# Larger experts in blocks of 1024 columns, gate before up, silu beside the down products

## The chip, the cores and the metric

The program runs on one core of one Trainium2 chip. Its time is the device time of one execution in microseconds (us); three executions of the kernel before gave a median of 1556.11 us (1555.88 to 1558.05). The three lie within 0.14% of each other.

## The reference

A bidirectional encoder of two layers over 256 tokens of width 1024. Each layer mixes the tokens and then applies a channel mixer: dense in layer 0, eight experts with two per token in layer 1. Only the experts matter here:

```python
def swiglu(h, w_gate, w_up, w_down):
    return (jax.nn.silu(h @ w_gate) * (h @ w_up)) @ w_down

def moe_swiglu(h, router, w_gate, w_up, w_down):
    logits = (t @ router); top_val, top_idx = lax.top_k(logits, 2); gates = softmax(top_val)
    combine = sum(one_hot(top_idx, 8) * gates[..., None], axis=1)
    for e in range(8):
        out = out + combine[:, e:e+1] * swiglu(t, w_gate[e], w_up[e], w_down[e])
```

`w_gate` and `w_up` are 1024 x 3584 for each expert, `w_down` is 3584 x 1024, all float32: 44 MB an expert, 352 MB in all, which is four fifths of what the program reads.

## The kernel before, in words

**Order of experts.** The tokens of an expert are gathered by matmuls with one-hot matrices. Experts run in pairs. Slots 0 and 1 are fixed; the other six experts are sorted by size at run time, so that slots 2, 4 and 6 hold at most 64 tokens ("few") and slots 3, 5 and 7 up to 128. Slots 0, 1, 3, 5 and 7 are the "larger" experts of the title. Below, (3, 1) is block 1 of slot 3.

**Loads.** SyncE (SP) issues every weight load, 512 KB each, into a ring of slots of 128 x 1024 floats; a load waits until what the slot held before has been read. A larger expert takes 28 loads of the gate matrix, 28 of up and 28 of down. In `wgu` a load of gate or up is 2 x 128 features by 512 columns, so each row of it in HBM is 2 KB long; a load of down is 128 features by 1024, rows of 4 KB. A few expert already takes 1024 columns at a time.

**Splits.** A larger expert is computed to nearly float32 by three float32r products. `wload` splits each load: ScalarE (ACT) rounds it into `whi` (line 200), VectorE (DVE) subtracts into `wlo` (line 208). There are five buffers of each. `mm3` then issues (x high, w high), (x high, w low), (x low, w high). Each load of a larger expert feeds six matmuls of 512 columns. A few expert uses its loads unsplit (`plain`, line 183) in float32.

**Blocks.** A larger expert goes in seven blocks of 512 columns. `gateup` interleaves gate and up: eight loads, one PSUM bank for each of the two (tag `pg`, four banks). After it come the down products of the block before (`down`, four loads). What lies between is put in by `between(k2)`, called four times in a `gateup`:

- `silu` at step 0: ACT takes silu of the gate bank (line 1650), DVE multiplies by the up bank (line 1651), for the block before
- `turn` at step 2: TensorE (PE) transposes the result in four pieces (line 229)
- `turned` at the first down load: ACT and DVE split the transposed result into `mah` and `mal` (lines 1698, 1699)
- generators in `side`: `combine` adds a finished expert's output to `y` (1742, 1743, 1753; for a few expert 1684, 1693), `gather` collects the tokens of the next pair (1600 to 1603), from block `GC0` = 2 of slots 1, 3 and 5.

PE executes in the order in which the code is written. ACT and DVE are ordered when the program is built: `behind_split` only says that a step may not stand ahead of the split of the newest load. Every engine then executes its own list in order.

Of the kernel before, what the change touches and what calls it, by code (L numbers as in the profile page):

```python
# [98 lines left out]
GC0 = 2  # L99
WARM = (7, 5)  # L100
SILU, TURN, TURNED = 0, 2, 1
ZPOOL = ((0, 0), (0, 1))
LAST = (0, 0, 0)


class K:
# [857 lines left out]
    def outproj(self, l, P, ks, first, last):  # L964
# [23 lines left out]
        if last:  # L988
            self.wn = None
            if l == 0:  # L990
                sq = P.tile([128, D], F32, name="nsq", tag="us")
                fT = self.mc.tile([128, 2, KD, T], F32R, name="fT", tag="G")
                self.norm_start(ROW_FFN + 8 * l, (fT[:, 0], fT[:, 1]))
                half = lambda a: self.norm_part((a,), (("pr", "pr", "pr", "py"), ("pq", "pq", "at", "at"))[a])
                self.ahead.append(self.wload(self.A["ffn_gate"][l // 2].rearrange("(k p) c -> p k c", p=128)[:, 0:2, 0:512], 2, 512))
            else:
                self.norm_start(None, None)
                xT = self.mc.tile([128, KD, T], F32, name="xT", tag="G")
                rt = P.tile([128, 512], F32, name="router", tag="gw")
# [6 lines left out]
                wgu = [self.A[n][l // 2, 0].rearrange("(k p) c -> p k c", p=128) for n in ("exp_gate", "exp_up")]  # L1006
                for n_ in range(NAHEAD):
                    self.early = [nc.gpsimd]
                    self.ahead.append(self.wload(wgu[n_ % 2][:, n_ // 2 * 2:n_ // 2 * 2 + 2, 0:512], 2, 512))
# [337 lines left out]
    def moe(self, l, P):  # L1347
# [47 lines left out]
        NB = DFF // 512  # L1395
# [32 lines left out]
        for n_ in range(len(ahead), XSPLIT + 3):  # L1428
            self.early = [nc.gpsimd if n_ in EPOOL else nc.vector]
            self.lo_after = self.pow if n_ > 3 else None  # L1430
            ahead.append(wgu(0, 0, n_ // 2, n_ % 2))
# [19 lines left out]
        def keep_clock(n):  # L1451

            for _ in range(n):
                self.mm(idle, w0[:, 0, :128], w0[:, 0], start=True, stop=True)
# [80 lines left out]
        def run(places, first):  # L1535
# [73 lines left out]
            def gateup(e, c0, between):  # L1609
                gh, gl, gs = G[e // 2]  # L1610
                bs = [self.bank("pg") for _ in range(2)]
                s0 = (e % 2) * 128 if gs is None else 0
                for k2 in range(KD // 2):
                    for s in range(2):
                        wh, wl = wgu(e, c0, k2, s)
                        for j in range(2):
                            k = 2 * k2 + j
                            self.mm3(bs[s], gh[:, k, s0:s0 + 128], gl[:, k, s0:s0 + 128], wh[:, j], wl[:, j],
                                     k == 0, k == KD - 1, False)
                    between(k2)  # L1620
                return bs

            def gateup_few(e, c0, between):
# [4 lines left out]
                n = 512 if c0 < DFF // 1024 else 256  # L1628
# [14 lines left out]
                return [b[:, :n] for b in bs]  # L1643

            def silu(e, bs):

                n = bs[0].free_size()
                sl = two("msilu", F32)[:, :n]
                rs = RS[e // 2][:, e % 2:e % 2 + 1]
                nc.scalar.activation(sl, bs[0], AF.Silu, scale=rs)  # L1650
                nc.vector.scalar_tensor_tensor(sl, bs[1], rs, sl, op0=ALU.mult, op1=ALU.mult)
                return sl
# [13 lines left out]
            def down_few(e, c0, operand, acc, beside):  # L1666
                n = 4 if c0 < DFF // 1024 else 2
                at = None
                for f in range(2 * n):
                    w = self.plain(wd[expert(e)][:, c0 * 8 + f:c0 * 8 + f + 1], 1, 1024)  # L1670
                    if not f:
                        with self.behind_split():
                            at = operand()
                    h, f_ = f // n, f % n
                    for hf in range(2):
                        self.mm(acc[64 * hf:64 * hf + 64], at[:, f_ * 128 + h * 64:f_ * 128 + h * 64 + 64], w[:, 0, hf * 512:hf * 512 + 512],
                                start=c0 == 0 and f == 0, stop=c0 == DFF // 1024 and f == 2 * n - 1, skip_group_check=True)
                    if f % 2:
                        beside(f // 2)
# [22 lines left out]
            def down(e, c0, operand, acc, beside):  # L1702
                ws = []
                for f in range(4):
                    ws.append(self.wload(wd[expert(e)][:, c0 * 4 + f:c0 * 4 + f + 1], 1, 1024))
                    if f < TURNED - 1:
                        continue
                    if f == TURNED - 1:
                        with self.behind_split():
                            ah, al = operand()  # L1710
                    for f_ in range(f + 1 if f == TURNED - 1 else 1):
                        one_down(f if f > TURNED - 1 else f_, c0, ah, al, acc, ws)
                    beside(f)

            def one_down(f, c0, ah, al, acc, ws):
                wh, wl = ws[f]
                for hf in range(2):
                    self.mm3(acc[hf], ah[:, f * 128:f * 128 + 128], al[:, f * 128:f * 128 + 128],
                             wh[:, 0, hf * 512:hf * 512 + 512], wl[:, 0, hf * 512:hf * 512 + 512],
                             c0 == 0 and f == 0, c0 == NB - 1 and f == 3, False)  # L1720

            def finish(e, c0, operand, accs, side, beside=lambda f: None):
                if few(e):
                    if c0 == 0:
                        accs[e] = self.bank("py")
                    down_few(e, c0, operand, accs[e], beside)
                    if c0 == DFF // 1024:
                        side.append(combine_few(e, accs[e]))
                    return
                if c0 == 0:  # L1730
                    accs[e] = [self.bank("py") for _ in range(2)]
                down(e, c0, operand, accs[e], beside)
                if c0 == NB - 1:
                    side.append(combine(e, accs[e]))
# [20 lines left out]
            def last(f):  # L1755

                if f == LAST[0]:
                    st["s"] = silu(NE - 1, st["n"])
                if f == LAST[1]:
                    st["t2"] = turn(st["s"])  # L1760
                if f == LAST[2]:
                    st["o"] = turned(st["t2"])

# [9 lines left out]
            seq = [(e, c0) for e in range(NE) for c0 in range(DFF // 1024 + 1 if few(e) else NB)]  # L1773
            if first:
                side.append(turns())
            for n_, (e, c0) in enumerate(seq):
                def between(k2):
                    with self.behind_split():
                        side[:] = [g for g in side if next(g, 0) is None]
                        if not n_:  # L1780
                            if first and k2 == GATES:
                                with self.tc.issue_after(self.gl):
                                    gates()
                            return
# [4 lines left out]
                st["n"] = bs = (gateup_few if few(e) else gateup)(e, c0, between)  # L1789
                if n_:  # L1790
                    finish(*seq[n_ - 1], lambda: (turned_few if few(seq[n_ - 1][0]) else turned)(st["t"]), accs, side, last if n_ == len(seq) - 1 else lambda f: None)
                elif first:
                    self.after = None
                st["b"] = bs
# [5 lines left out]
            finish(*seq[-1], lambda: st["o"], accs, side)  # L1800
# [114 lines left out]
```

## Time and profile before

| | |
|---|---|
| median of three runs | 1556.11 us |
| the profiled execution | 1553.22 us, span 1551.4 us |
| PE / DVE / ACT busy over the span | 94% / 65% / 52% |
| granted TensorE clock, mean | 0.978 of full |
| experts | from about 645 us to 1536 us |

A row of the chain of waits is a start, a length and what ran, followed back from the last instruction. A row of the timeline is a start, the length of one or of several, engine, line, operation, output and inputs, and in square brackets how long the engine had been idle and what it had waited for. Matmul ends are modelled; the distance from one start to the next is the real pace.

### The profile page before, as it was taken

How to read it: one execution, taken by the hardware profiler on the slowest of the kernel's cores; microseconds unless marked ns; L12 is line 12 of the kernel's file. 1: busy time of each engine (PE TensorE's matmuls, PEld its weight loads, DVE VectorE, ACT ScalarE, POOL GpSimd, SP SyncE). 2: the span in 40 equal slices, each digit the busy share in tenths (PEclk: the TensorE clock that was granted, in tenths of full speed). 3: DMA queues.
4: the chain of work that ended last, by engine and by line, in shares of the span. 5: the costliest groups of instructions: out<-in, count | busy, mean ns of one | idle time of the engine just before them, and what ended most of it. 6: DMA issues, size and time to landing. Idle time of an engine off the chain costs nothing.

```text
span 1551.4 us, 27151 instructions
## 1 busy us (share of the span) xinstructions
PE 1463.6 (94%) x10215; PEld 1111.4 (72%) x10215; DVE 1003.6 (65%) x1314; ACT 806.2 (52%) x1142; POOL 178.4 (11%) x161
## 2 busy tenths in 40 slices
PE   7799989999998999799999999999998999998996
PEld 6677889999986778688888743588634687435885
DVE  5865665556659746698899720699512898205896
ACT  4545454444445354587878510687302776205785
POOL 2532100000026423300001000001000010000001
PEclk9899999999998899899999999999999999999998
DMA  7322356666543230899999999999999999999991
GB/s 230 104 70 98 109 166 188 186 182 189 163 120 95 70 125 3 310 412 410 338 332 348 353 407 415 410 411 413 403 419 412 410 411 412 389 416 411 410 413 43
DMA packets 172457, 434.67 MB, mean 280 GB/s; under 512 B 14834, under 2 KB 18013, under 8 KB 172317
## 3 DMA queue, kind: packets, MB, share of 16 engines
q1 hardware_dynamic: 170924, 430.74, 74.4%
q8 instruction: 82, 1.34, 0.3%
q0 software_dynamic: 544, 1.12, 0.3%
q10 hardware_dynamic: 848, 0.99, 0.2%
q14 instruction: 59, 0.48, 0.1%
HBM read 431.75 MB, written 1.05 MB: 279 GB/s over the span
## 4 chain that ended last, share of the span: by engine, by line
PE 75%; DVE 9%; DMA 7%; ACT 3%; issue 3%; POOL 1%; ACTq 0%; SPq 0%; DVEq 0%; POOLq 0%
PE ps L225 72%; PE ps L229 3%; DMA r<-in_exp_up 2%; DMA raw<-in_exp_up 2%; DMA r<-in_exp_gate 2%; DVE wlo L208 2%; DVE wlox L208 1%; DMA posi<-in_positions 1%; ACT whi L200 1%; ACT whix L200 0%; DVE AR L655 0%; DMA x<-in_x 0%; DVE us L550 0%; DVE kd L659 0%; ACT Sf L761 0%
## 5 line engine op out<-in xcount | busy, mean ns | idle before, releaser
L208 DVE TENSOR_TENSOR wlo<-r,whi 128x1024 fp32r<-128x1024 f32 x192 | 234.6, 1248 | 42.3 <-ACT whi L200 41.1
L200 ACT CAST whi<-r 128x1024 fp32r<-128x1024 f32 x195 | 201.0, 1056 | 37.5 <-DMA r<-in_exp_gate 19.3
L208 DVE TENSOR_TENSOR wlox<-r,whix 128x1024 fp32r<-128x1024 f32 x120 | 147.1, 1246 | 65.3 <-ACT whix L200 64.2
L200 ACT CAST whi<-raw 128x1024 fp32r<-128x1024 f32 x119 | 124.7, 1052 | 97.4 <-PE ps L225 82.6
L208 DVE TENSOR_TENSOR wlo<-raw,whi 128x1024 fp32r<-128x1024 f32 x104 | 129.7, 1251 | 59.7 <-ACT whi L200 59.3
L200 ACT CAST whix<-r 128x1024 fp32r<-128x1024 f32 x120 | 124.5, 1056 | 36.9 <-DMA r<-in_exp_gate 25.1
L225 PE MATMUL ps<-whi,gf 128*128 128x512 f32 x400 | 137.2, 401 | 1.3 <-ACT whi L200 1.3
L225 PE MATMUL ps<-r,gs 128*64 128x512 f32 (+1 forms) x636 | 130.6, 541 | 2.6 <-DMA r<-in_exp_up 2.5
L225 PE MATMUL ps<-fT,whi 128*128 128x256 f32 x544 | 100.8, 287 | 4.7 <-DVE gu L1306 3.7
L1417 POOL TENSOR_TENSOR xp<-x,xp 128x512 fp32r<-128x512 f32 x12 | 24.3, 2026 | 631.6 <-ACT xp L1416 631.6
L225 PE MATMUL ps<-whix,gf 128*128 128x512 f32 x272 | 93.9, 400 | 2.5 <-ACT whix L200 2.5
L225 PEld LDWEIGHTS ps<-r,gs 128*64 128x64 f32 x636 | 42.8, 136 | 74.1 <-issue 58.3
L225 PEld LDWEIGHTS ps<-whi,gf 128*128 128x128 f32 x400 | 76.6, 191 | 21.9 <-ACT whi L200 2.9
L225 PEld LDWEIGHTS ps<-fT,whi 128*128 128x128 f32 x544 | 86.2, 194 | 6.0 <-issue 4.3
L1663 ACT COPY mah<-ps 128x512 f32<-128x512 f32 (+1 forms) x12 | 6.4, 532 | 143.9 <-PE ps L229 143.9
L225 PE MATMUL ps<-wlo,gf 128*128 128x512 f32 x200 | 79.6, 398 | 1.2 <-DVE wlo L208 1.1
L225 PE MATMUL ps<-fT,wlo 128*128 128x256 f32 x272 | 77.6, 285 | 0.0
L225 PE MATMUL ps<-whi,hT_h 128*128 128x512 f32 x160 | 69.6, 435 | 5.6 <-DVE up L1073 5.5
L208 DVE TENSOR_TENSOR wlox<-raw,whix 128x1024 fp32r<-128x1024 f32 x51 | 63.1, 1242 | 17.5 <-ACT whix L200 16.6
L225 PE MATMUL ps<-r,mah 128*64 128x512 f32 x276 | 64.8, 599 | 2.4 <-DMA r<-in_exp_down 2.0
L225 PE MATMUL ps<-whi,mah 128*128 128x512 f32 x170 | 66.5, 391 | 0.0
L225 PE MATMUL ps<-wlo,mah 128*128 128x512 f32 x170 | 66.4, 390 | 0.0
(468 smaller groups left out, 3400.3 us busy)
## 6 DMA issues: line engine op xcount, KB each, us to landing
r<-in_exp_down SPq DMA_DIRECT2D x178, 512.0 KB, 10.1
r<-in_exp_up SPq DMA_DIRECT2D x172, 512.0 KB, 10.0
r<-in_exp_gate SPq DMA_DIRECT2D x172, 512.0 KB, 10.0
raw<-in_exp_gate SPq DMA_DIRECT2D x43, 512.0 KB, 10.0
raw<-in_exp_up SPq DMA_DIRECT2D x43, 512.0 KB, 9.9
raw<-in_exp_down SPq DMA_DIRECT2D x37, 512.0 KB, 10.0
raw<-in_w_in_first SPq DMA_DIRECT2D x22, 512.0 KB, 4.3
raw<-in_w_in_rest SPq DMA_DIRECT2D x22, 512.0 KB, 3.6
```

The source lines that it names most:

```text
L200: w1 = nc.scalar.copy(hi[:, :a * b], raw[:, :a * b])
L208: w2 = (early or nc.vector).tensor_sub(lo[:, :a * b], raw[:, :a * b], hi[:, :a * b].bitcast(F32))
L225: self.nc.tensor.matmul(out, lhsT, rhs, start=start, stop=stop, skip_group_check=skip_group_check)
L229: self.nc.tensor.transpose(out, in_, ident)
L1417: nc.gpsimd.tensor_sub(xl, xs, xh.bitcast(F32))
L1663: nc.scalar.copy(at, b)
```

## The change

A larger expert goes in three blocks of 1024 columns and one of 512. A block of 1024 computes all of gate first, into two banks, and then all of up, into two more; its loads are 128 features by 1024 columns. `between` is called once every two loads. `silu` of a block no longer stands in the `gateup` after it but directly behind the first load of the down products that follow its own `gateup` (those of the block before); it is now two steps, silu on ACT and `times` on DVE, one of each per bank. The transposes come at steps 0 and 1 of the next `gateup`, the splits of them at steps 1 and 2. `gather` now starts after block 0. Few experts keep their blocks but follow the same order of steps. Line numbers are lower by 3 up to line 1400 or so, and move by up to 20 behind it.

```diff
-        NB = DFF // 512
+        NB = DFF // 1024 + 1
...
-        def wgu(e, c0, k2, s):
+        def wgu(e, c0, s, k):
             if ahead and first_run[0]:
                 return ahead.pop(0)
-            return self.wload((wg, wu)[s][expert(e)][:, 2 * k2:2 * k2 + 2, c0 * 512:c0 * 512 + 512], 2, 512)
+            w = (wg, wu)[s][expert(e)]
+            if c0 < NB - 1:
+                return self.wload(w[:, k:k + 1, c0 * 1024:c0 * 1024 + 1024], 1, 1024)
+            return self.wload(w[:, 2 * k:2 * k + 2, c0 * 1024:c0 * 1024 + 512], 2, 512)
...
             def gateup(e, c0, between):
...
-                bs = [self.bank("pg") for _ in range(2)]
...
-                for k2 in range(KD // 2):
-                    for s in range(2):
-                        wh, wl = wgu(e, c0, k2, s)
+                n = 2 if c0 < NB - 1 else 1
+                bs = st["n"] = [[], []]
+                for s in range(2):
+                    bs[s].extend(self.bank("pg") for _ in range(n))
+                    for i in range(KD * n // 2):
+                        wh, wl = wgu(e, c0, s, i)
                         for j in range(2):
...
+                            k, h = (i, j) if n == 2 else (2 * i + j, 0)
...
+                        if i % 2:
+                            between(s * (KD * n // 4) + i // 2)
...
             def silu(e, bs):
...
+                sls = []
+                for b in bs:
+                    sls.append(two("msilu", F32)[:, :b.free_size()])
+                    nc.scalar.activation(sls[-1], b, AF.Silu, scale=RS[e // 2][:, e % 2:e % 2 + 1])
+                return sls
+
+            def times(e, sls, bs):
+                for sl, b in zip(sls, bs):
+                    nc.vector.scalar_tensor_tensor(sl, b, RS[e // 2][:, e % 2:e % 2 + 1], sl, op0=ALU.mult, op1=ALU.mult)
...
+            def down(e, c0, ops, acc, beside):
+                n = 4 * len(ops)
+                for f in range(n):
+                    wh, wl = self.wload(wd[expert(e)][:, c0 * 8 + f:c0 * 8 + f + 1], 1, 1024)
+                    ah, al = ops[f // 4]
...
                     beside(f)
...
+            def turn_step(e, i):
+
+                if 0 < i <= len(st["s"]):
+                    st["o"].append((turned_few if few(e) else turned)(st["t"]))
+                if i < len(st["s"]):
+                    st["t"] = turn(st["s"][i])
...
-                        if k2 == SILU:
-                            st["s"] = silu(seq[n_ - 1][0], st["b"])
-                        elif k2 == TURN:
-                            st["t"] = turn(st["s"])
+                        if not step:
+                            st["o"] = []
+                        turn_step(seq[n_ - 1][0], step)
+
+                def beside(f):
+                    with self.behind_split():
+                        if not f:
+                            st["s"] = silu(e, st["n"][0])
+                            times(e, st["s"], st["n"][1])
+                        if end and f > 2:
+                            if f == 3:
+                                st["o"] = []
+                            turn_step(e, f - 3)
...
-                if (e, c0) == (NE - 1, GC0):
+                if (e, c0) == (NE - 1, 0):
...
-                if e % 2 and e < NE - 1 and c0 == GC0:
+                if e % 2 and e < NE - 1 and c0 == 0:
                     side.append(gather(e // 2 + 1))
```

How the steps stand on DVE, in slot 0. In these rows `wlo` with a number is the low half of one load in the order of the program, `msilu` the product of silu and up, `ps` a PSUM bank. Before, at block 4: `ps461` is its up bank, last written from load 470; loads 471 to 474 are down loads, 477 and 478 the first of the next block.

```order
L208 TENSOR_TENSOR wlox470_7936<-raw470_7934,whix470_7935 128x1024
L208 TENSOR_TENSOR wlox471_7948<-myh_7946,whix471_7947 128x1024
L1699 TENSOR_TENSOR mal_7499<-ps468_7918,mah_7498 128x512
L208 TENSOR_TENSOR wlo472_7962<-myl_7960,whi472_7961 128x1024
L208 TENSOR_TENSOR wlo473_7974<-r8_7972,whi473_7973 128x1024
L208 TENSOR_TENSOR wlo474_7986<-y_7984,whi474_7985 128x1024
L208 TENSOR_TENSOR wlox477_7999<-y_7984,whix477_7998 128x1024
L208 TENSOR_TENSOR wlox478_8011<-raw478_8009,whix478_8010 128x1024
L1651 SCALAR_TENSOR_TENSOR msilu_7412<-ps461_7844,rs_7291,msilu_7412 128x512
```

The multiplication stands six splits behind the load that last wrote its up bank.

In the change, the same engine at block 2 of slot 0: `ps467` and `ps468` are its two up banks, last written from load 476; load 477 is the first down load.

```order
L205 TENSOR_TENSOR wlo475_7976<-r8_7974,whi475_7975 128x1024
L205 TENSOR_TENSOR wlo476_7988<-y_7986,whi476_7987 128x1024
L205 TENSOR_TENSOR wlox477_7999<-y_7986,whix477_7998 128x1024
L1660 SCALAR_TENSOR_TENSOR msilu_7461<-ps467_7902,rs_7291,msilu_7461 128x512
L1660 SCALAR_TENSOR_TENSOR msilu_7461<-ps468_7903,rs_7291,msilu_7461 128x512
L205 TENSOR_TENSOR wlox478_8015<-raw478_8013,whix478_8014 128x1024
```

The two multiplications stand one split behind that load, and ahead of the split of load 478.

What PE does there in the change: the last three matmuls of each up bank, then the down products of loads 477 and 478.

```order
L222 MATMUL ps467_7902<-whi476_7987,gl0_7218 128x512
L222 MATMUL ps468_7903<-whi476_7987,gh0_7217 128x512
L222 MATMUL ps468_7903<-wlo476_7988,gh0_7217 128x512
L222 MATMUL ps468_7903<-whi476_7987,gl0_7218 128x512
L222 MATMUL ps445_7688<-whix477_7998,mah_7539 128x512
L222 MATMUL ps445_7688<-wlox477_7999,mah_7539 128x512
L222 MATMUL ps445_7688<-whix477_7998,mal_7540 128x512
L222 MATMUL ps446_7689<-whix477_7998,mah_7539 128x512
L222 MATMUL ps446_7689<-wlox477_7999,mah_7539 128x512
L222 MATMUL ps446_7689<-whix477_7998,mal_7540 128x512
L222 MATMUL ps445_7688<-whix478_8014,mah_7539 128x512
L222 MATMUL ps445_7688<-wlox478_8015,mah_7539 128x512
```

Where `ps461` was followed by four down loads and two of the next block before its multiplication was due, the second matmul of load 478 now needs a split that stands behind the multiplications. In block 1 of slot 0 (and of slots 3, 5 and 7) three splits stand ahead of them instead of one:

```order
L205 TENSOR_TENSOR wlox444_7678<-r19_7676,whix444_7677 128x1024
L205 TENSOR_TENSOR wlox447_7692<-r18_7690,whix447_7691 128x1024
L205 TENSOR_TENSOR wlo448_7708<-r1_7706,whi448_7707 128x1024
L205 TENSOR_TENSOR wlo449_7720<-r2_7718,whi449_7719 128x1024
L1660 SCALAR_TENSOR_TENSOR msilu_7461<-ps435_7595,rs_7291,msilu_7461 128x512
```

Here load 444 was the last of up, and the multiplication moved behind the splits of the down loads 447 to 449.

## Rows read from the trace of the kernel before

**Rows 1.** The page: span, busy times of the engines, GB/s in 40 slices.

```profile
span 1551.4 us, 27151 instructions
PE 1463.6 (94%) x10215; PEld 1111.4 (72%) x10215; DVE 1003.6 (65%) x1314; ACT 806.2 (52%) x1142; POOL 178.4 (11%) x161
GB/s 230 104 70 98 109 166 188 186 182 189 163 120 95 70 125 3 310 412 410 338 332 348 353 407 415 410 411 413 403 419 412 410 411 412 389 416 411 410 413 43
```

**Rows 2.** Windows: length, busy PE, PEld, DVE, ACT, POOL; clock; DMA share; GB/s.

```profile
660.00:760.00 100.00, 100.00 (x454) 82.71 (x453) 91.57 (x92) 80.72 (x86) 0.00 (x0) 1.00 1.04 411
760.00:900.00 140.00, 139.47 (x649) 108.90 (x649) 116.18 (x116) 96.22 (x122) 9.76 (x4) 1.00 0.93 332
900.00:950.00 50.00, 50.00 (x228) 19.24 (x226) 10.63 (x13) 7.24 (x11) 0.00 (x0) 1.00 1.03 419
1100.00:1120.00 20.00, 20.00 (x98) 9.01 (x97) 6.52 (x8) 5.54 (x7) 0.00 (x0) 1.00 1.01 388
```

**Rows 3.** The timeline of PE at the start of slot 3.

```profile
975.54 0.50 PE L225 MATMUL ps<-wlo,gf 128*128 128x512 f32 x1 [0.76 <-DVE wlo L208]
...
1004.14 0.66 PE L229 MATMUL ps<-ident,msilu 128*128 128x128 f32 x4 [0.84 <-DVE y L1693]
```

**Rows 4.** The chain of waits in the experts: start, length, what ran.

```profile
669.62 16.38 PE ps L225 x72
...
719.63 0.44 PE ps L229 x4
...
963.28 9.88 DMA r<-in_exp_gate
...
992.49 0.69 ACT msilu L1650
```

**Rows 5.** The timeline of DVE in slot 0.

```profile
720.72 0.69 DVE L1699 TENSOR_TENSOR mal<-ps,mah 128x512 fp32r<-128x512 f32 x1 [1.47 <-ACT mah L1698]
721.66 1.23 DVE L208 TENSOR_TENSOR wlo<-myl,whi 128x1024 fp32r<-128x1024 f32 x1 [0.25 <-ACT whi L200]
722.81 1.22 DVE L208 TENSOR_TENSOR wlo<-r,whi 128x1024 fp32r<-128x1024 f32 x1
```

**Rows 6.** The timeline of ACT in slot 0.

```profile
728.32 1.06 ACT L200 CAST whi<-r 128x1024 fp32r<-128x1024 f32 x1 [0.30 <-PE ps L225]
```

**Rows 7.** Issues on SP at the end of slot 2; of exp_gate from the page.

```profile
953.00 1.63 SPq L183 DMA_DIRECT2D r<-in_exp_down  x2
...
963.28 0.38 SPq L197 DMA_DIRECT2D r<-in_exp_gate  x1
...
973.28 4.18 SPq L183 DMA_DIRECT2D r<-in_exp_down  x4
...
r<-in_exp_gate SPq DMA_DIRECT2D x172, 512.0 KB, 10.0
```

**Rows 8.** The timeline of PE in the last block of slot 7.

```profile
1524.17 0.39 PE L225 MATMUL ps<-whix,gf 128*128 128x512 f32 x1
...
1525.76 0.60 PE L229 MATMUL ps<-ident,msilu 128*128 128x128 f32 x4
1526.11 0.47 PE L225 MATMUL ps<-whi,mah 128*128 128x512 f32 x1
1526.60 0.50 PE L225 MATMUL ps<-wlo,mah 128*128 128x512 f32 x1
```

**Rows 9.** The timeline of DVE at the same place.

```profile
1524.66 0.75 DVE L1651 SCALAR_TENSOR_TENSOR msilu<-ps,rs,msilu 128x512 f32<-128x512 f32 x1 [1.54 <-PE ps L225]
1525.33 2.35 DVE L208 TENSOR_TENSOR wlo<-r,whi 128x1024 fp32r<-128x1024 f32 x2
```

**Rows 10.** The timeline of PE in the first block of slot 0.

```profile
650.52 0.61 PE L225 MATMUL ps<-sel,one 128*128 128x8 f32 x4 [1.06 <-DVE rs L1571]
```

**Rows 11.** Windows behind that wait and behind the one of rows 3.

```profile
652.00:656.00 4.00, 4.00 (x12) 3.18 (x11) 3.24 (x11) 1.64 (x2) 0.00 (x0) 0.57 1.04 407
1004.00:1008.00 4.00, 3.86 (x19) 3.27 (x20) 4.00 (x6) 2.88 (x4) 0.00 (x0) 1.00 1.06 409
```

More of the change, by code (lines that the diff above doesn't have):

```diff
@@ L98 @@
 GSTEP, GATES = 4, 1
-GC0 = 2
 WARM = (7, 5)
-SILU, TURN, TURNED = 0, 2, 1
 ZPOOL = ((0, 0), (0, 1))
-LAST = (0, 0, 0)
 class K:
@@ L1005, in outproj @@
                 nc.gpsimd.tensor_mul(rt[:, :, :NE], rt[:, :, :NE], gain[:, :, None].to_broadcast([128, KD, NE]))
-                wgu = [self.A[n][l // 2, 0].rearrange("(k p) c -> p k c", p=128) for n in ("exp_gate", "exp_up")]
+                wgu = [self.A["exp_gate"][l // 2, 0].rearrange("(k p) c -> p k c", p=128)]
                 for n_ in range(NAHEAD):
                     self.early = [nc.gpsimd]
-                    self.ahead.append(self.wload(wgu[n_ % 2][:, n_ // 2 * 2:n_ // 2 * 2 + 2, 0:512], 2, 512))
+                    self.ahead.append(self.wload(wgu[0][:, n_:n_ + 1, 0:1024], 1, 1024))
                 lt = self.bank("py")
@@ L1430, in moe @@
             self.lo_after = self.pow if n_ > 3 else None
-            ahead.append(wgu(0, 0, n_ // 2, n_ % 2))
+            ahead.append(wgu(0, 0, 0, n_))
             if n_ == 3:
@@ L1453, in keep_clock @@
             for _ in range(n):
-                self.mm(idle, w0[:, 0, :128], w0[:, 0], start=True, stop=True)
+                self.mm(idle, w0[:, 0, :128], w0[:, 0, :512], start=True, stop=True)
         keep_clock(WARM[0])
@@ L1627, in gateup_few @@
                 bs = [self.bank("pg") for _ in range(2)]
-                n = 512 if c0 < DFF // 1024 else 256
+                n = 512 if c0 < NB - 1 else 256
+                st["n"] = [[b[:, :n]] for b in bs]
                 for k2 in range(KD // 2):
@@ L1664, in turned_few, with down_few @@
                 return at
-            def down_few(e, c0, operand, acc, beside):
-                n = 4 if c0 < DFF // 1024 else 2
-                at = None
+            def down_few(e, c0, ops, acc, beside):
+                n = 4 if c0 < NB - 1 else 2
                 for f in range(2 * n):
                     w = self.plain(wd[expert(e)][:, c0 * 8 + f:c0 * 8 + f + 1], 1, 1024)
-                    if not f:
-                        with self.behind_split():
-                            at = operand()
                     h, f_ = f // n, f % n
                     for hf in range(2):
[L1676 to L1679, printed above, removed]
+                        self.mm(acc[64 * hf:64 * hf + 64], ops[0][:, f_ * 128 + h * 64:f_ * 128 + h * 64 + 64], w[:, 0, hf * 512:hf * 512 + 512],
+                                start=c0 == 0 and f == 0, stop=c0 == NB - 1 and f == 2 * n - 1, skip_group_check=True)
+                    beside(f)
             def combine_few(e, acc):
@@ L1700, in turned @@
                 return ah, al
[L1702 to L1712, printed above, removed]
-                    beside(f)
@@ L1715, in one_down @@
[L1715 to L1729, printed above, removed]
+            def down(e, c0, ops, acc, beside):
[3 more added lines that the diff above has]
+                    ah, al = ops[f // 4]
+                    f_ = slice(f % 4 * 128, f % 4 * 128 + 128)
+                    for hf in range(2):
+                        self.mm3(acc[hf], ah[:, f_], al[:, f_], wh[:, 0, hf * 512:hf * 512 + 512], wl[:, 0, hf * 512:hf * 512 + 512],
+                                 c0 == 0 and f == 0, c0 == NB - 1 and f == n - 1, False)
+                    beside(f)
@@ L1730, in finish @@
+            def finish(e, c0, ops, accs, side, beside=lambda f: None):
                 if c0 == 0:
-                    accs[e] = [self.bank("py") for _ in range(2)]
-                down(e, c0, operand, accs[e], beside)
+                    accs[e] = self.bank("py") if few(e) else [self.bank("py") for _ in range(2)]
+                (down_few if few(e) else down)(e, c0, ops, accs[e], beside)
                 if c0 == NB - 1:
-                    side.append(combine(e, accs[e]))
+                    side.append((combine_few if few(e) else combine)(e, accs[e]))
@@ L1754, in combine @@
                         yield
[L1755 to L1762, printed above, removed]
             G = {}
@@ L1772, in run, with between @@
             accs, st = {}, {}
-            seq = [(e, c0) for e in range(NE) for c0 in range(DFF // 1024 + 1 if few(e) else NB)]
+            seq = [(e, c0) for e in range(NE) for c0 in range(NB)]
             if first:
                 side.append(turns())
+            def turn_step(e, i):
[3 more added lines that the diff above has]
+                    st["t"] = turn(st["s"][i])
             for n_, (e, c0) in enumerate(seq):
-                def between(k2):
+                end = n_ == len(seq) - 1
+                def between(step):
                     with self.behind_split():
@@ L1780, in between @@
                         if not n_:
-                            if first and k2 == GATES:
+                            if first and step == GATES:
                                 with self.tc.issue_after(self.gl):
                                     gates()
+                            if step == KD - 2:
+                                st["s"] = silu(e, st["n"][0])
                             return
-                        if k2 == SILU:
-                            st["s"] = silu(seq[n_ - 1][0], st["b"])
-                        elif k2 == TURN:
-                            st["t"] = turn(st["s"])
@@ L1789, in run @@
-                st["n"] = bs = (gateup_few if few(e) else gateup)(e, c0, between)
-                if n_:
[L1791 to L1794, printed above, removed]
-                if (e, c0) == (NE - 1, GC0):
+                        if not step:
+                            st["o"] = []
+                        turn_step(seq[n_ - 1][0], step)
@@ new lines, in beside @@
+                def beside(f):
+                    with self.behind_split():
+                        if not f:
+                            st["s"] = silu(e, st["n"][0])
+                            times(e, st["s"], st["n"][1])
[3 more added lines that the diff above has]
+                            turn_step(e, f - 3)
+                (gateup_few if few(e) else gateup)(e, c0, between)
+                if n_:
+                    finish(*seq[n_ - 1], st["o"], accs, side, beside)
+                else:
+                    with self.behind_split():
+                        times(e, st["s"], st["n"][1])
+                    if first:
+                        self.after = None
```

17 lines of the change are left out of this document (4 added, 13 removed).

## The prediction, written before the change was run

> **What bounds the kernel now.** I read the page first, then windows along the experts, the chain of waits, and last the timelines of PE, DVE, ACT and SP where the change moves steps. PE is busy 94% of the span and the transfers run at 410 GB/s in most slices of the experts [rows 1], so the share of busy time doesn't say which of the two ends last. The windows do [rows 2]. In 660 to 760 PE has no gap, and the transfers run at 411 GB/s. In 760 to 900 (slots 0 and 1, both larger) PE still has only half a microsecond of gap in 140, and the transfers fall to 332: the ring is full and SP waits for PE. In 900 to 950 (slot 2, few) they are back at 419; PE is shown busy all the time, but it works as loads land: at 975.54, early in slot 3, a split was late for it [rows 3], and the chain goes through a landing of exp_gate that took 9.88 us at 963.28 [rows 4]. In 1100 to 1120 (end of slot 3) the rate dips to 388: the ring is full again, just.
>
> So from the end of a few expert to the moment at which the ring is full the time is PE's, from there to the end of the next few expert it is the transfers'. What PE loses while the larger expert runs is lost for good, as long as the ring is full when that expert ends. A gain of the transfers counts only behind that point, which is in a few expert.
>
> PE's own pace: 72 matmuls in 16.38 us in the chain [rows 4] are 0.2275 us each, so 6 x 0.2275 = 1.365 us a load. DVE makes a split in 722.81 - 721.66 = 1.15 us [rows 5], and ACT stands idle 0.30 us for PE ahead of a split [rows 6]: both run ahead until the five buffers are full. With 1.365 - 1.15 = 0.21 us won a load, it takes DVE five loads or so to win back one lost microsecond.
>
> **What doesn't change.** The number of matmuls, splits, transposes, silus and bytes is the same. 240 of the 280 loads of gate and up have rows of 4 KB where they had 2 KB.
>
> **The rows of the loads.** An issue on SP waits for the load eight before it (10.0 us from issue to landing [rows 7]). The issues at 953.00, 963.28 and 973.28 are eight loads apart: 10.28/8 = 1.285 us for those of 2 KB, 10.00/8 = 1.250 for those of 4 KB. 240 x 0.035 = 8.4 us of transfer go. But the stretches that the transfers limit hold mainly loads of few experts, which keep their form, and the larger expert beside them has PE as its limit. I take 0; the ends are 0 and -8.4.
>
> The Trainium skill (DMA: Bandwidth & Descriptors, Specifications) says that a transfer goes at line rate from 512 bytes on; by that this term is 0 at both ends. The trace shows 0.035 us of difference a load instead, in one pair of issues [rows 7].
>
> **The added wait, the main term.** `times` is now on DVE behind the split of the first down load and ahead of that of the second. It needs the last matmul of up; DVE has run ahead, and stands. Behind it stand the splits, and for the first of them PE comes 7 matmuls after that last matmul of up (six of the first down load, one of the second). Before, six splits stood between, and nothing waited.
>
> The trace has this order once: in the last block, where `last` already put silu behind the first down load. The last matmul of up starts at 1524.17 [rows 8] and so ends at 1524.40; the multiplication starts 0.27 us later at 1524.66, after 1.54 us of idle for PE, and the split stands behind it at 1525.33 [rows 9], 0.67 on. PE goes on with that split at 1526.60 [rows 8]. Wanted it was at 1524.40 + 7 x 0.2275 = 1525.99: 0.61 us late. A block of 1024 has two multiplications, one more by 0.67, but its first bank is done three matmuls (0.68 us) earlier: 0.61 again. If both wait for the end, 0.67 more in the seven wide ones of the places below, +4.7 in all. Lower end: 0, if the transfers set the time there anyway; a gain is excluded, since no work leaves PE.
>
> Where it holds, by the changed order of DVE: in (0,2), (0,3), (1,0), (1,1), (1,2), (1,3), (2,0), and in (3,2), (3,3), (4,0) and the like of slots 5 and 6, and (7,2), (7,3). That is 7 + 3 + 3 + 2 = 15 places. In block 1 of slots 0, 3, 5 and 7 three splits stand ahead of the multiplications, so PE has 19 matmuls (4.3 us) where 2.8 are needed: nothing. In (3,0), (5,0) and (7,0) the down loads are of a few expert and are not split. 15 x 0.61 = +9.2 us.
>
> **Turned.** The split of the transposed result stands two loads ahead of its use. In the trace the transposes end at 719.63 + 0.44 = 720.07 [rows 4], `mal` starts at 720.72 after 1.47 us of idle, and the second split behind it starts at 721.66 + 1.15 = 722.81 [rows 5]. The first split behind `mal` ends at 721.66 + 1.23 = 722.89, so 2.82 us after the transposes. PE now comes for it after two loads and a matmul, 2 x 1.365 + 0.2275 = 2.96. It fits, by 0.14 us. I take 0; if it is missed by as much, 19 blocks x 0.14 = +2.7. A gain isn't there.
>
> **Gather and combine.** `gather` starts in block 1, not 3, and now meets `combine` of the expert before in (1,1), (3,1) and (5,1). The trace shows nothing of the two together. Nearest is a wait of PE for the `y` of combine, 0.84 us at 1004.14 [rows 3]. I take half of it, 3 x 0.4 = +1.2; the ends are 0 and two such waits each, 3 x 2 x 0.84 = +5.0.
>
> **Silu leaves the valley.** At the start of slots 3, 5 and 7, where PE has nothing in hand, the silu of the few expert's last block is in the chain (0.69 us at 992.49 [rows 4]). It now runs earlier, under down loads. I take 3 x -0.7 = -2.1; ends 0 and -3. In the last block the transposes no longer stand between two down loads; the wait behind them, 1526.60 - (1526.11 + 0.23) = 0.26 us [rows 8], goes: -0.3. The four banks of a wide block are all free again one or two loads into the down products, ahead of the next gate: 0.
>
> **Sum.** 9.2 + 0 + 0 + 1.2 - 2.1 - 0.3 = +8.0. The profiled execution took 1553.22 us, so 1561.2; the median of the three runs stands 2.9 above it: 1564.1 us.
>
> **Rivals.** What can be told from no change here is about 0.2%, 3.1 us.
>
> *Faster: the transfers set the time all along.* Then PE's stalls vanish in the ring, and 8.4 us of the loads come back: 1556.1 - 8.4 = 1547.7. For it speaks the rate of 410 or more in nearly every slice of the second half [rows 1]; against it 332 GB/s over 140 us with PE full, and the dip to 388 [rows 2].
>
> *No change: stalls count only in slots 0 and 1.* The dip to 388 is so shallow that in slots 3 to 7 the ring may not be full at the end. Then 7 places stay, 4.3 - 2.1 - 0.3 + 0.4 = +2.3: 1558.4.
>
> *Much slower: the clock.* After the wait of 1.06 us at 650.52 [rows 10] PE had a granted clock of 0.57 on average in 652 to 656 (between the levels of 1.2 and 2.4 GHz): 12 matmuls took 4.00 us [rows 11] where 12 x 0.2275 = 2.73 do, 1.3 us lost. If each of the 15 stalls brought this: 15 x 1.3 = 19 more, 1583. Against it, behind the wait of 0.84 at 1004.14 [rows 3] the granted clock stayed at 1.00 [rows 11], the level of 2.4 GHz. The Trainium skill (TensorE: Matmul & The Clock Gate, "A second HAM failure mode: psum-queue depth-cycling") tells of a kernel whose clock swung because PE idled briefly between groups of matmuls; by it the 1583 would be the forecast, by the second window of rows 11 it is not.
>
> *Slower by more: the stalls are longer.* Both multiplications wait for the end (+4.7) and `turned` is missed (+2.7): 1571.5. The row of the tail has one multiplication, so it can't exclude this.
>
> **How the numbers follow.** Forecast 0.52; faster 0.18; no change 0.18; longer stalls 0.08; clock 0.04. The forecast's own range is 1560 to 1570. It and the two slower rivals make slower, 0.52 + 0.08 + 0.04 = 0.64; faster 0.18, same 0.18. The range from 1549 to 1573 takes in the no-change case and the longer stalls, and all but the end of the faster one; it leaves out the clock.
>
> **What would show it.** *The wait:* rows of the multiplication on DVE with idle time put down to PE, behind them PE idle about 0.6 us for a `wlo` at the 15 places, and PE no longer full in 660 to 760. The chain should then show DVE's msilu and wlo between the matmuls. *The ring:* the time from the start of slot 0 to the end of slot 1 longer by some 4 us, the few experts as long as before. *Turned:* no idle of PE at the first down load of a block. *The loads:* eight issues of gate loads 10.0 us apart also in slot 3. The forecast is wrong if PE shows no idle at those places, if such idle is there but the start of slot 2 stands where it stood, or if the time from slot 3 on shrinks by more than slots 0 and 1 lose.

## The result, and the profile after

The changed kernel took 1568.15 us (median of 6 runs, 1562.98 to 1573.37) beside 1557.07 us for the kernel before: a ratio of 1.0066 (ratios here are those of the means; the medians differ by 11.1 us), 95% interval 1.0046 to 1.0085, or 7 to 13 us more. The forecast was 8.0 us more, 1564, in a range of 1549 to 1573. In a second set of runs the same kernel came out at 1.0055 (1.0042 to 1.0068), 6.5 to 10.6 us.

The page of the kernel after: span, PE, and GB/s in 40 slices.

```profile
span 1561.9 us, 27150 instructions
PE 1466.1 (94%) x10215; PEld 1111.1 (71%) x10215; DVE 1000.7 (64%) x1314; ACT 812.2 (52%) x1142; POOL 177.1 (11%) x161
GB/s 227 106 70 97 108 162 182 185 187 189 162 112 101 69 124 3 321 419 417 287 324 349 342 395 415 419 419 415 355 419 416 420 416 396 393 416 419 419 416 40
```

PE still shows 94% [rows 1], and its 10215 matmuls are the same; from such shares the loss can't be read. The windows answer to [rows 2]. The kernel after reaches the same place in the program 4 to 12.5 us later than the kernel before, so the second and third window end where the few expert's first matmul begins, in slot 2 and in slot 4. The kernel after:

```profile
660.00:760.00 100.00, 99.08 (x446) 81.04 (x445) 88.87 (x93) 80.01 (x85) 0.00 (x0) 1.00 1.03 417
763.85:896.91 133.06, 130.55 (x601) 106.18 (x599) 115.82 (x116) 97.10 (x120) 10.61 (x4) 1.00 0.88 312
1094.10:1114.10 20.00, 19.54 (x87) 15.53 (x87) 15.74 (x16) 12.23 (x14) 0.00 (x0) 1.00 0.94 337
```

The second and third in the kernel before:

```profile
760.00:886.84 126.84, 126.31 (x582) 103.55 (x580) 114.79 (x114) 94.20 (x118) 9.76 (x4) 1.00 0.93 329
1081.60:1101.60 20.00, 20.00 (x95) 16.41 (x93) 16.92 (x18) 12.67 (x18) 3.06 (x1) 1.00 1.03 417
```

PE has gaps where it had none: 0.92 us in the first window (0.00 before), 2.51 in the second (0.53 before), while the transfers, with a full ring, wait more than before (312 GB/s for 329, and at the end of slot 3 337 for 417).

The gap at one of the 15 places, block 2 of slot 0. PE, timeline, columns as in [rows 8]; the `whi,gl` is the last matmul of up:

```profile
731.78 0.39 PE L222 MATMUL ps<-whi,gl 128*128 128x512 f32 x1
...
733.36 0.39 PE L222 MATMUL ps<-whix,mah 128*128 128x512 f32 x1
734.21 0.50 PE L222 MATMUL ps<-wlox,mah 128*128 128x512 f32 x1 [0.46 <-DVE wlox L205]
734.55 0.40 PE L222 MATMUL ps<-whix,mal 128*128 128x512 f32 x1
```

DVE at the same place:

```profile
731.59 1.43 DVE L1660 SCALAR_TENSOR_TENSOR msilu<-ps,rs,msilu 128x512 f32<-128x512 f32 x2 [2.51 <-PE ps L222]
732.94 1.21 DVE L205 TENSOR_TENSOR wlox<-raw,whix 128x1024 fp32r<-128x1024 f32 x1
```

And the chain of waits there:

```profile
731.59 0.64 DVE msilu L1660
...
732.94 1.22 DVE wlox L205
734.16 0.04 issue
734.21 12.35 PE ps L222 x53
```

DVE has run ahead, stands 2.51 us, multiplies twice, and only then makes the split. It begins the split 0.93 us after the last matmul of up (731.78 + 0.23 = 732.01), as in the tail of before: 1525.33 - 1524.40 = 0.93 [rows 8, 9]. From one start to the next PE takes 734.21 - 733.36 = 0.85 us, 0.62 more than its pace of 0.23; the step behind it is 0.34 instead of 0.23, a further 0.11. PE shows such a step of `wlo` in the down products at 15 places: 11 of 0.62, one of 0.72, and three of 0.48 at the first blocks of slots 2, 4 and 6. The sum is 8.98 us, or 10.6 with the 0.11 behind each.

Where the 10.5 us between the two profiled spans stand is read from PE's first matmul of slots 0, 3, 5 and 7 and the first of the last combine. In the kernel before:

```profile
645.17 0.50 PE L225 MATMUL ps<-whi,gh 128*128 128x512 f32 x1 [0.52 <-DVE gl L1603]
974.28 0.50 PE L225 MATMUL ps<-whi,gf 128*128 128x512 f32 x1 [1.29 <-ACT whi L200]
1189.30 0.51 PE L225 MATMUL ps<-whix,gf 128*128 128x512 f32 x1 [1.24 <-ACT whix L200]
1405.47 0.50 PE L225 MATMUL ps<-whix,gf 128*128 128x512 f32 x1 [1.24 <-ACT whix L200]
1536.34 0.50 PE L225 MATMUL ps<-myh,PT 128*128 128x512 f32 x1
```

In the kernel after:

```profile
649.02 0.50 PE L222 MATMUL ps<-whi,gh 128*128 128x512 f32 x1 [0.52 <-DVE gl L1604]
984.56 0.50 PE L222 MATMUL ps<-whi,gf 128*128 128x512 f32 x1 [1.26 <-ACT whi L197]
1202.04 0.50 PE L222 MATMUL ps<-whix,gf 128*128 128x512 f32 x1 [1.24 <-ACT whix L197]
1417.36 0.49 PE L222 MATMUL ps<-whix,gf 128*128 128x512 f32 x1 [1.21 <-ACT whix L197]
1547.69 0.50 PE L222 MATMUL ps<-myh,PT 128*128 128x512 f32 x1
```

The differences are +3.9 ahead of the experts, +6.4 in slots 0 to 2, +2.5 in 3 and 4, -0.9 in 5 and 6, -0.5 in 7, and -0.9 behind. Two of these are not the change's waits. The first lies in the dense stage, where the clock falls at other places from run to run; in the ten traces the experts start between 645.17 and 651.32, at 645.97 to 650.03 with the change's early loads and at 645.17 to 651.32 with those of before. And in slots 5 and 7 the granted clock fell in the kernel before but not after (0.72 against 1.00, the mean of 6 us). The windows of the kernel before there:

```profile
1190.00:1196.00 6.00, 5.44 (x17) 4.32 (x18) 5.85 (x7) 5.01 (x7) 0.00 (x0) 0.72 1.05 411
1406.00:1412.00 6.00, 5.27 (x16) 4.23 (x17) 5.80 (x7) 5.20 (x6) 0.00 (x0) 0.72 1.05 404
```

Those of the kernel after:

```profile
1203.00:1209.00 6.00, 5.70 (x26) 4.60 (x26) 5.17 (x6) 4.92 (x7) 0.00 (x0) 1.00 1.02 418
1418.00:1424.00 6.00, 5.38 (x25) 4.42 (x26) 5.16 (x5) 4.93 (x7) 0.00 (x0) 1.00 1.02 417
```

The matmuls went 0.43 apart in place of 0.23 for 3.4 us there, at a granted clock of 0.50 (1.2 GHz), so such a drop costs about 1.7 us by estimate. Stages are compared below only where both or neither had one.

### The profile page after: what moved, and what is told of

Same layout as the page of the kernel before. It is cut to its first block, busy times and chain, and to the rows that moved or that the text cites. A ratio compares the mean times of both kernels' runs of the same rounds, so it can differ in the third digit from the quotient of the medians.

```text
span 1561.9 us, 27150 instructions
## 1 busy us (share of the span) xinstructions
PE 1466.1 (94%) x10215; PEld 1111.1 (71%) x10215; DVE 1000.7 (64%) x1314; ACT 812.2 (52%) x1142; POOL 177.1 (11%) x161
## 4 chain that ended last, share of the span: by engine, by line
PE 71%; DVE 11%; DMA 9%; ACT 3%; issue 3%; POOL 2%; ACTq 0%; SPq 0%; DVEq 0%; POOLq 0%
PE ps L222 69%; DMA r<-in_exp_up 4%; DVE wlo L205 3%; DMA r<-in_exp_gate 3%; PE ps L226 2%; DVE wlox L205 2%; DMA posi<-in_positions 1%; DMA raw<-in_exp_gate 1%; ACT whi L197 1%; DMA raw<-in_exp_down 1%; ACT whix L197 0%; DVE kd L656 0%; DMA x<-in_x 0%; ACT Sf L758 0%; DVE us L546 0%
## 5 line engine op out<-in xcount | busy, mean ns | idle before, releaser
L197 ACT CAST whi<-r 128x1024 fp32r<-128x1024 f32 x199 | 206.0, 1056 | 47.7 <-DMA r<-in_exp_gate 23.0
L197 ACT CAST whi<-raw 128x1024 fp32r<-128x1024 f32 x115 | 120.8, 1052 | 100.3 <-PE ps L222 88.4
L205 DVE TENSOR_TENSOR wlox<-r,whix 128x1024 fp32r<-128x1024 f32 x119 | 143.8, 1229 | 25.5 <-ACT whix L197 24.8
L222 PE MATMUL ps<-whi,gf 128*128 128x512 f32 x392 | 132.8, 399 | 1.3 <-ACT whi L197 1.3
L1660 DVE SCALAR_TENSOR_TENSOR msilu<-ps,rs,msilu 128x512 f32<-128x512 f32 (+1 forms) x47 | 33.2, 732 | 123.6 <-PE ps L222 74.8
L1655 ACT ACTIVATE msilu<-ps,rs 128x512 f32<-128x512 f32 (+1 forms) x47 | 30.1, 676 | 101.7 <-PE ps L222 101.7
L197 ACT CAST whix<-raw 128x1024 fp32r<-128x1024 f32 x52 | 54.7, 1054 | 23.8 <-PE ps L222 23.4
```

The lines of the kernel that those rows point to most:

```text
L197: w1 = nc.scalar.copy(hi[:, :a * b], raw[:, :a * b])
L205: w2 = (early or nc.vector).tensor_sub(lo[:, :a * b], raw[:, :a * b], hi[:, :a * b].bitcast(F32))
L222: self.nc.tensor.matmul(out, lhsT, rhs, start=start, stop=stop, skip_group_check=skip_group_check)
L1655: nc.scalar.activation(sls[-1], b, AF.Silu, scale=RS[e // 2][:, e % 2:e % 2 + 1])
L1660: nc.vector.scalar_tensor_tensor(sl, b, RS[e // 2][:, e % 2:e % 2 + 1], sl, op0=ALU.mult, op1=ALU.mult)
```

## The experiments

Eight kernels ran, each beside the kernel before: 1, 2, 3 and 7 on one chip, where the kernel before took 1555.98 us, and 4, 5, 6 and 8 on another, where it took 1556.40. The ratios go to the kernel before on the same chip.

**1. The changed kernel again.** No edit.

> The changed kernel once more, unaltered, as the standard of this chip. Theory (waits of DVE): about 10 us above the kernel before (1.0066), with PE standing 0.62 us for a split at 12 places of slots 0, 1, 3, 5 and 7 and 0.48 at the three first blocks of the few experts. The first expert started 3.9 us later than before in the profile of the changed kernel, in code that the change hardly touches. Theory (clock, by chance): that start lies now on this side, now on that of 645 us. Rival (the early loads of the first expert cost time): it lies near 649 again, and near 645 in the kernels that load it as before.

1564.62 us, 1.0055 (1.0042 to 1.0068). The trace has the same 15 places, 8.98 us in sum. Its experts start at 647.61, between the two values, and kernels 3, 7 and 8, with the loads of before, start at 649.60 to 651.32. So the early loads are out as the reason.

**2. Silu behind the third down load.**

```diff
-                        if not f:
+                        if f == 2:
                             st["s"] = silu(e, st["n"][0])
```

> The changed kernel with silu and its multiplication put in behind the third down load in place of the first. Theory (the wait on DVE makes the loss): the places have three splits ahead of the multiplication, PE comes for the fourth 4.3 us after the last product of up, the 15 gaps go and the time falls by 15 x 0.61 = 9.2 us against the changed kernel, to within 2 us of the kernel before. Rival (wide blocks, the two-step turn or the earlier gather make it): it stays some 10 us above the kernel before. Rival (ring): half of it goes, since only the stalls of slots 0 and 1 count.

1555.74 us, 1.0004 (0.9992 to 1.0016): 8.9 us less than the changed kernel beside it (7.9 by the two ratios), and no different from the kernel before. Blocks of 1024, the turn in two steps and the earlier gather are all still there, so together they are not the loss. Groups of PE's instructions in the experts (line, names, count | busy, mean ns | idle before, releaser), in the kernel after:

```profile
L222 PE MATMUL ps<-wlo,mah 128*128 128x512 f32 x161 | 63.8, 397 | 3.7 <-DVE wlo L205 3.7
...
L222 PE MATMUL ps<-wlox,mah 128*128 128x512 f32 x108 | 42.8, 396 | 2.9 <-DVE wlox L205 2.9
```

In this one:

```profile
L222 PE MATMUL ps<-wlo,mah 128*128 128x512 f32 x168 | 65.6, 391 | 0.1
...
L222 PE MATMUL ps<-wlox,mah 128*128 128x512 f32 x112 | 43.6, 389 | 0.0
```

The idle time ahead of `wlo` in the down products, 6.6 us, is gone (0.1; the row's idle is smaller than the step because the ends of matmuls are modelled). One place keeps a step 0.3 us too long, in (1,2) at 860.23. On DVE the multiplications of block 2 no longer wait:

```profile
728.96 1.22 DVE L205 TENSOR_TENSOR wlo<-r,whi 128x1024 fp32r<-128x1024 f32 x1
730.11 1.40 DVE L1660 SCALAR_TENSOR_TENSOR msilu<-ps,rs,msilu 128x512 f32<-128x512 f32 x2
731.43 2.35 DVE L205 TENSOR_TENSOR wlo<-r,whi 128x1024 fp32r<-128x1024 f32 x2
```

**3. The kernel before with silu behind the first down load.**

```diff
+                def early(f):
+                    if f == 0:
+                        with self.behind_split():
+                            st["m"] = silu(e, st["n"])
...
-                            st["s"] = silu(seq[n_ - 1][0], st["b"])
+                            st["s"] = st["m"] if n_ > 1 else silu(seq[n_ - 1][0], st["b"])
...
-    finish(..., last if n_ == len(seq) - 1 else lambda f: None)
+    finish(..., last if n_ == len(seq) - 1 else early)
```

> The kernel before, with blocks of 512 and its own loads, but silu and its multiplication moved behind the first down load for every block. Theory (the place of the multiplication alone makes the loss): by the order on DVE 23 places more have one split ahead of it, 23 x 0.61 = 14 us, less 2 for silu leaving the chain of the valleys: 12 us slower than the kernel before. Rival (the loss comes from the wide blocks or the other loads): within 3 us of the kernel before. Rival (clock): more than 25 us slower.

1570.46 us, 1.0091 (1.0077 to 1.0106), 12 to 16.5 us: the place of the multiplication alone, with neither wide blocks nor new loads. The trace has 23 places more, 14.6 us in sum (21 of them at 0.47 to 0.62, one of 0.75, one of 1.20). One of them on PE:

```profile
745.31 0.39 PE L225 MATMUL ps<-whi,mah 128*128 128x512 f32 x1
746.16 0.50 PE L225 MATMUL ps<-wlo,mah 128*128 128x512 f32 x1 [0.46 <-DVE wlo L208]
```

And on DVE:

```profile
744.22 0.75 DVE L1651 SCALAR_TENSOR_TENSOR msilu<-ps,rs,msilu 128x512 f32<-128x512 f32 x1 [1.53 <-PE ps L225]
744.89 1.21 DVE L208 TENSOR_TENSOR wlo<-r,whi 128x1024 fp32r<-128x1024 f32 x1
```

With one multiplication the step is the same 0.85 us (746.16 - 745.31) as with two in the wide blocks: the first of two does run while the second bank is being finished.

**4. A second DVE instruction in the wait.**

```diff
                     nc.vector.scalar_tensor_tensor(sl, b, ..., sl, op0=ALU.mult, op1=ALU.mult)
+                    nc.vector.tensor_tensor(sl, sl, sl, op=ALU.max)
```

> The changed kernel with one more DVE instruction of 128 x 512 behind each multiplication (a maximum of the product with itself, which leaves the values as they are). Theory (PE waits for what stands on DVE ahead of the split): each stall grows by the instruction, about 0.6 us, in 8 places, and by two of them, 1.2 us, in the 7 places of wide blocks: 13 us slower than the changed kernel, with gaps of 1.2 and 1.8 us on PE. Rival (the gap is the trip from PE to DVE and back, whatever DVE does): the gaps stay at 0.62 and the time within 2 us of the changed kernel.

1569.08 us, 1.0080 (1.0061 to 1.0099); against the changed kernel (1.0055) 4 us more, not 13. In six of the seven wide blocks the step grew as expected (in (1,1) by half of it). Block 2 of slot 0 on PE:

```profile
734.70 0.39 PE L222 MATMUL ps<-whix,mah 128*128 128x512 f32 x1
736.75 0.50 PE L222 MATMUL ps<-wlox,mah 128*128 128x512 f32 x1 [1.67 <-DVE wlox L205]
```

And on DVE:

```profile
732.93 1.43 DVE L1660 SCALAR_TENSOR_TENSOR msilu<-ps,rs,msilu 128x512 f32<-128x512 f32 x2 [2.52 <-PE ps L222]
734.28 1.28 DVE L1661 TENSOR_TENSOR msilu<-msilu 128x512 f32<-128x512 f32 x2
735.48 1.22 DVE L205 TENSOR_TENSOR wlox<-raw,whix 128x1024 fp32r<-128x1024 f32 x1
```

2.05 - 0.23 = 1.82 us late, 1.20 more than 0.62, and the two maxima take 735.48 - 734.28 = 1.20. So PE waits for whatever DVE has ahead of the split, and the trip there and back is not the price. The miss of the time has its reason in the order on DVE: in the narrow blocks the maximum was put behind the next split, and in three of them the multiplication too slipped one split back, where PE waits no more. The steps sum to 16.5 us, 7.5 more, which the interval of the difference of the two ratios (0.3 to 7.5 us) only just holds.

**5 and 6. The wait left in one half.** Silu behind the third down load in slots 0 to 2, and in slots 3 to 7.

```diff
-                        if not f:
+                        if f == (2 if e < 2 or (e, c0) == (2, 0) else 0):    # 5
+                        if f == (0 if e < 2 or (e, c0) == (2, 0) else 2):    # 6
```

> The changed kernel with silu and its multiplication behind the third down load in slots 0, 1 and at the first block of slot 2 only; the 8 places of slots 3 to 7 keep the wait. Theory (every stall counts, as PE fills the ring in each larger expert): those 8 stalls are 6 x 0.62 + 2 x 0.48 = 4.7 us, and with the 0.11 that the matmul behind each adds some 5.5: 5 us slower than the kernel before and 4 faster than the changed kernel. Rival (the ring hides stalls in slots 3 to 7): the same as the kernel before.

> The complement: the wait stays at the 7 places of slots 0 to 2, and goes in slots 3 to 7. Theory: 4.3 us of stalls, with 0.11 each behind them 5: some 5 us slower than the kernel before. Rival (the ring hides stalls in slots 3 to 7): all of the loss stays, 9 us.

Kernel 5 took 1558.41 us, 1.0015 (0.9999 to 1.0032); kernel 6 1559.35, 1.0020 (1.0006 to 1.0034). Both lie below the 5 us expected, which is at the edge of either interval. All nine microseconds in slots 0 to 2 are excluded by kernel 6; that the stalls of 3 to 7 are free is not excluded by the time of kernel 5 alone. The lengths of the stages, from PE's starts as above, are sharper, though each is of one trace (us; * with a drop of the clock):

| | slots 0-2 | 3, 4 | 5, 6 | 7 |
|---|---|---|---|---|
| before | 329.11* | 215.02* | 216.17* | 130.87* |
| after | 335.54* | 217.48* | 215.32 | 130.33 |
| 2, no wait | 329.25 | 215.26* | 215.10* | 130.39* |
| 5, wait in 3 to 7 | 331.68* | 215.50 | 216.69* | 131.74* |
| 6, wait in 0 to 2 | 335.44* | 215.98* | 214.91* | 130.36* |

Like with like: slots 0 to 2, 6 less 5, 3.8 us for steps of 4.0; slots 3 and 4, after less 2, 2.2 for steps of 1.7 and 0.3 behind them; slots 5 and 6, 5 less 2, 1.6 for 1.7; slot 7, 5 less 2, 1.35 for 1.24 and 0.2. Where two traces have the same program and the same clock, a stage differs by up to 0.7 us (slots 3 and 4 of 2 and 6). Within that the steps count in full, in the later slots too; whether the 0.11 behind each counts can't be told.

**7 and 8. The old loads.** Wide blocks with loads of 256 features by 512 columns, first with the wait, then with silu behind the third down load.

```diff
...
-                return self.wload(w[:, k:k + 1, c0 * 1024:c0 * 1024 + 1024], 1, 1024)
+                c = c0 * 1024 + k % 2 * 512
+                return self.wload(w[:, k // 2 * 2:k // 2 * 2 + 2, c:c + 512], 2, 512)
...
```

> The changed kernel, but the wide blocks load 256 features by 512 columns again (rows of 2 KB), the two halves of a block in turn; all else as changed, the waits too. Theory (the row width is worth nothing, since PE sets the time where these loads stand): the same as the changed kernel within 2 us. Rival (4 KB rows gain 0.035 us a load and hide a larger loss): 8.4 us slower than the changed kernel.

> The changed kernel with silu behind the third down load and with loads of 256 features by 512 columns (rows of 2 KB) in the wide blocks: against the same with 4 KB rows it differs in the loads alone, with no wait left in either. Theory (PE sets the time where these loads stand): the same within 1.5 us. Rival (0.035 us a load count): 8.4 us slower than with 4 KB rows.

7 took 1562.70 us, 1.0042 (1.0029 to 1.0055): 1.9 less than the changed kernel, inside the 2 expected, but for a reason that was not foreseen. Only 11 of the 15 places are left, 6.5 us: in (0,2), (1,1), (3,2) and (5,2) the second of the two multiplications came one split later. 8 has no such difference and decides: 1557.15 us, 1.0003 (0.9990 to 1.0015), beside 1.0004 for kernel 2. The 8.4 us of the rival are out: the difference of the two ratios is 0 within 2.7 us. The transfers do go faster with rows of 4 KB; in the first full slice of slot 0 (the 18th) kernel 2 moves 419 GB/s, kernel 8 410. The row of the page, kernel 2:

```profile
GB/s 231 104 71 97 109 169 183 188 183 186 162 117 97 57 138 2 290 419 416 318 347 333 353 403 416 419 420 415 379 419 416 419 415 405 391 416 419 419 413 35
```

Kernel 8:

```profile
GB/s 226 108 69 98 109 163 182 186 188 189 164 106 95 70 138 2 268 410 413 331 341 336 359 391 416 410 410 414 403 418 411 411 410 418 402 416 410 410 415 50
```

The stages show what the times can't. In the order of the table they are 334.75*, 215.48, 215.17 and 131.94* us in kernel 7 and 331.11*, 215.22, 215.20 and 129.44 in kernel 8. In slots 0 to 2 the stalls of 7 count: 3.6 us for steps of 2.8 and 0.5 behind them. In slots 3 to 6 they do not: 0.3 and 0.0 us, for steps of 1.1 and 0.2 behind them in either pair. In kernel 8, with rows of 2 KB, the ring is not full there when the larger expert ends: in the 20 us ahead of slot 4's first matmul the transfers of kernel 2 are held back a little, those of kernel 8 are not (ahead of slot 6 it is 393 and 419 GB/s). So what PE lost could come back in the few expert. With more stalls they count again: in kernel 3, with rows of 2 KB and ten stalls in those slots, 4.7 us of 6.2. A window of kernel 2:

```profile
1086.30:1106.30 20.00, 20.00 (x94) 16.34 (x93) 16.42 (x16) 12.89 (x15) 0.00 (x0) 1.00 1.02 404
```

Of kernel 8:

```profile
1089.80:1109.80 20.00, 20.00 (x92) 16.39 (x92) 16.48 (x16) 12.95 (x15) 0.00 (x0) 1.00 1.03 419
```

And in slots 3 to 6 kernel 8 without a drop of the clock takes as long as kernel 2 with one. So where the clock does not fall, the wider rows may be worth up to the 1.7 us of a drop in either pair of slots; with one trace each this is not shown.

## Why the prediction was right

- **What bounds the kernel.** Right for the changed kernel: stalls of PE in a larger expert are lost in full (5 and 6), and faster loads beside it gain nothing that the times show (8). The stretch from slot 0's first matmul to slot 1's last down product takes 268.49 us, 263.18 before: 5.3 more, where some 4 were expected. But the prediction took loads and stalls as separate terms, and they hang together: its condition, a full ring when the larger expert ends, is met in slots 3 to 6 with the rows of 4 KB, and with those of 2 KB it is not, unless more stalls hold PE up (8 and 7, against 3). The 2% that the loads gain, 419 to 410 GB/s, stand beside the 2.8% that the pair of issues gave, 1.285 to 1.250. The Trainium skill (DMA: Bandwidth & Descriptors, Specifications) has every transfer from 512 bytes on at line rate; in rate the traces differ from that (419 to 410), and in time no run shows a difference.
- **The added wait, +9.2.** Right in place, count and price: 15 places; 0.62 us where 0.61 was expected, though 0.48 at the few experts, where PE's step from the first down product to the second is 0.33 in place of 0.23 (911.54 to 911.87) and PE so comes later for the split; 8.98 in sum. Left out was the slower step behind each (0.11, some 1.7 together). The upper end for wide blocks (+4.7) isn't reached.
- **Turned, 0.** Right: no place of the first down loads shows a gap for it.
- **Silu out of the valley, gather, tail: -1.2 together.** Not tested one by one. Kernel 2 less before, at the same clock, is +0.2, -1.1 and -0.5 in slots 3 to 7, -1.3, where -1.6 was expected of these slots. The meeting of gather and combine shows up as a wait of PE for `rs`, 0.25 us at 876.04 and once more each in slots 3 and 5; the wait of 0.84 us for `y` is in both kernels. What silu in the valley cost PE is a wait of 0.30 us at three places of the kernel before, a step of 0.69 for 0.23, and in the kernel after it is gone: 0.46 each, where 0.7 was taken. The first of them:

```profile
995.43 0.50 PE L225 MATMUL ps<-wlo,gf 128*128 128x512 f32 x1 [0.30 <-DVE wlo L208]
```

- **Not foreseen: some 2 us in slots 0 to 2.** With no wait, these take 331.7 (5) at the clock of before, which took 329.1. About 1.0 of them lies behind the last down product of slot 1 (66.9 us to the first matmul of slot 3 in kernel 2, 65.9 before and 65.8 in kernel 3); between the two one load more lands (47 for 46) in every kernel with blocks of 1024. Why is open. Kernel 2 is still no slower than before as a whole.
- **Rivals.** Faster by the loads: out (8). No change since the ring hides the later stalls: out by the stages for the changed kernel, though so it is in slots 3 to 6 with the old loads (7). Clock: out; in ten traces no stall of 0.6 to 1.8 us in the larger experts is followed by a drop. The swing that the Trainium skill (TensorE: Matmul & The Clock Gate, "A second HAM failure mode: psum-queue depth-cycling") tells of is shown by no run here at such stalls. Longer stalls: out, with 0.62 in the wide blocks and none for `turned`.

The size came out larger in the first runs (10.3 us) than in the second (8.6); the sum of 8.0 stands inside either interval.

With the wait removed (2), the rest of the change neither gains nor loses anything that these runs can tell.

## What to carry to other kernels

An engine that executes in order and runs ahead is a queue: a step put behind "the newest" piece of work waits for the slowest producer, and all that stands behind waits with it. Count how many pieces stand between the last producer and the waiting step, and how many between it and its consumer; here one split ahead cost 0.62 us at a larger expert and 0.48 at a few, and three cost nothing but 0.3 us at one place. A place in the kernel that already has the same order gives the price. Whether the price is paid depends on the transfers: it came back where the ring was not yet full (7, slots 3 to 6).

## What the runs showed of the hardware

After the same pause at the start of slots 3, 5 and 7 (PE idle for 1.2 to 1.3 us, and for 0.76 to 0.77 more one matmul later) the granted clock fell to the lower level, 1.2 GHz, in 20 of 30 places in the ten traces, for 3.4 us, and in the others not at all. The same holds at the first block of slot 0: behind the wait at 654.4 the clock fell in the kernel after, 0.60, and stayed at 1.00 in kernel 2. Windows, columns as in [rows 11], of the kernel after:

```profile
656.00:660.00 4.00, 4.00 (x13) 3.09 (x12) 3.08 (x11) 1.59 (x2) 0.00 (x0) 0.60 1.04 423
```

Of kernel 2:

```profile
656.00:660.00 4.00, 4.00 (x20) 3.29 (x19) 3.83 (x12) 2.81 (x3) 0.00 (x0) 1.00 1.03 420
```

In the other eight traces it fell there too. So one profile can differ from another by about 1.7 us at each such place without any change of the program.
